# A fused two-block transformer on one core: activations placed at the top of SBUF, weight slots picked by operand role, and six small tiles for the last stage's split gates

## The chip, the cores and the metric

The kernel runs on one core of a Trainium2 chip. The metric is the device time of one execution in microseconds, taken as the median of three runs. One further execution was recorded by the hardware profiler, and the rows in this document come from that one.

## What is computed

The reference is two model blocks in a row on 256 tokens of width 1024, all in float32. The first block is a SwiGLU layer, a mixer (stick-breaking attention and a state-space scan side by side), a cross attention on 256 memory rows, and a second SwiGLU layer. The second block is a convolution and a gated recurrence, and then a layer of 16,384 small experts, which takes nearly half of the time. Cut to that layer:

```python
q = (xt @ wq).reshape(t, PEER_HEADS, 2, HALF_Q)
scores = jnp.einsum('thpd,hpnd->thpn', q, keys)
...                                   # top 16 of 16 x 16 sums per head: expert ids and gates
def block(args):
    u = jnp.take(u_tab, eb, axis=0)
    a = gelu(jnp.einsum('td,thkd->thk', xb, u))
    w = gb * a
    vv = jnp.take(v_tab, eb, axis=0)
    return jnp.einsum('thk,thkd->td', w, vv)
```

The kernel doesn't gather. It multiplies all tokens with the whole table u, scales the result by a matrix of gates that is zero for experts not chosen, and multiplies that with the whole table v.

## The kernel before

All weights arrive as 533 *units* of 128 x 1024 floats, in the order in which they are needed. SyncE loads a unit into a raw buffer. `prefetch` then takes a free *slot*: ScalarE writes the rounded value into its `hi` tile (L142), VectorE the rest into its `lo` tile (L143). So each product of two floats becomes three matmuls (high x high, high x low, low x high) on operands that TensorE takes in one pass. Activations are split in the same way, into `uT0` (high) and `uT1` (low), or into blocks of the arena `ra`.

A matmul has two operands in SBUF: the one that is loaded into the array first (here called the *held* operand) and the one that is streamed through it. There are two ways to use a weight unit:

- `f_tile` (L305 to L307) holds the weights and streams the activations, 256 columns: 24 matmuls a unit. The projections that come out by feature use it, most of the SwiGLU units, 12 units of the experts' query (`pq`), and all 128 units of the u table (`pu`).
- `half_chunk` (L272 to L276) and `acc_step` (L322 to L326) hold the activations and stream the weights, 512 columns. The last 128 units (`pv`, the v table) are of this kind: 12 matmuls a unit into four accumulators.

There are eight slots in SBUF (`hi0`/`lo0` to `hi7`/`lo7`), two more in `ra` for a while, and only slots 0 to 3 from `pq` on. A slot becomes free when its unit has been used up (`release`); `prefetch` takes `max(slots)`.

Where a tile lies follows from the order in which the pools allocate. In KB from the start of a partition, by the program's own memory table:

| tile | before | after |
|---|---|---|
| `raw0`; `raw1`, `raw2` | 18; 22 to 30 | 18; 216 to 224 |
| slots 0 to 3 | 30 to 62 | 22 to 54 |
| `uT0`, `uT1` (activations) | 62 to 78 | 200 to 216 |
| slots 4 to 7 | 88 to 120 | 129 to 161 |
| `fa` (float32 arena) | 120 to 185 | 64 to 129 |
| `ra` (split arena, two extra slots) | 185 to 217 | 161 to 193 |
| `X` (experts' matrix, last stages) | 80 to 208 | 68 to 196 |
| `w0`, `w1` (first split gates) | 212 to 216 | 56 to 60 |
| `r00` to `r31` (split gates) | none | 60 to 68 |

Below, *low* means slots 0 to 3 and all else under 78 KB, and *high* means 86 KB and above; before, TensorE reads no matmul operand in between.

In the `pu` stage VectorE and GpSimd work beside TensorE: first they pick experts (`routing`), then `gates` builds 64 groups of gates and scales `X` with them. In the `pv` stage `wsplit(i + 4)` (L1473, L1474) splits the gated matrix `X` four units ahead, into the eight places of `uT`, which is free by then; units 0 and 1 use `w0`/`w1`.

The order of all instructions is the order in which this Python code issues them: each helper calls `tick`, which may call `prefetch` or a step of a side task.

Of the kernel before, what the change touches and what calls it, by code (L numbers as in the profile page):

```python
# [5 lines left out]
F32 = mybir.dt.float32  # L6
F32R = mybir.dt.float32r
# [8 lines left out]
D = 1024  # L16
# [3 lines left out]
UNITS = [("ff1", 66), ("v", 8), ("qk", 16), ("dt", 1), ("xs", 8), ("bc", 4), ("z", 8),  # L20
         ("mk", 8), ("wo1", 16), ("mv", 8), ("xq", 8), ("xo", 8), ("ff2", 66),
         ("v2", 4), ("g2", 4), ("f2", 4), ("q2", 4), ("chb", 12), ("wo2", 8),
         ("pq", 16), ("pu", 128), ("pv", 128)]
FIRST = {}
# [10 lines left out]
FFN_AT = {}  # L35
_n = 0
for _s in FFN_ORDER:
    FFN_AT[_s] = _n
    _n += 4 if _s[0] == "gu" else 2

COLS = [("ffn1_pre_g", 8), ("mix_pre_g", 8), ("xa_pre_g", 8), ("mem_g", 8), ("ffn2_pre_g", 8),
        ("norm_mix_2", 8), ("norm_ffn_2", 8), ("attn_norm_g", 8), ("ssd_norm_g", 8), ("conv_gain_2", 4),
# [9 lines left out]
ROWS = ["ffn1_post_g", "mix_post_g", "xa_post_g", "ffn2_post_g", "norm_f_2", "d_skip"]  # L52
# [48 lines left out]
class Builder:  # L101
    RAW = 3
    RING = (4, 4)

    def __init__(self, tc, io, dbg=None, stop=None):
        self.tc, self.nc, self.io = tc, tc.nc, io
# [6 lines left out]
        self.retired = False  # L113
        self.live = sum(self.RING)
        self.sides = []
# [11 lines left out]
    def prefetch(self, n=1):  # L127

        nc = self.nc
        self.load()  # L130
        while n > 0 and self.split_i < self.dma_i:
            i = self.split_i
            slots = [x for x in self.free if x < self.RING[0] or i < FIRST["pq"]]
            if not slots:
                return
            slot = max(slots)
            self.free.remove(slot)
            self.slot_of[i] = slot
            hi, lo = self.slots[slot]
            x = self.raw_of.pop(i)  # L140
            raw = self.raw[x]
            nc.scalar.activation(hi, raw, AF.Copy)  # L142
            nc.vector.tensor_sub(lo, raw, hi.bitcast(F32))  # L143
            self.split_i += 1
            if x < self.RAW or not self.retired:
                self.raw_free.append(x)
            else:
                self.raw_extra.pop(x).free()
            n -= 1
            self.load()  # L150
# [31 lines left out]
    def retire(self, slots=True):  # L182

        self.retired = True
        if slots:
            self.live = sum(self.RING)
        for slot in [x for x in self.free if x >= self.live]:
# [1150 lines left out]

    def gates(self, kT, X):

# [33 lines left out]

    def peer(self):
        nc, hT = self.nc, self.uT
        small_scope = self.tc.tile_pool(name="px", bufs=1)
        px = small_scope.__enter__()
        X = px.tile([128, 128, 256], F32, name="X")
        XA = Arena(X.rearrange("p i t -> p (i t)")[:, 40 * 256:], 88 * 256)  # L1380
        kT = px.tile([128, 4, 256], F32, name="kT")
# [83 lines left out]
                self.u_done = i + 1  # L1465
            return f
        self.routed = False
        w01 = tuple(px.tile([128, 2, 256], F32R, name=f"w{i}") for i in range(2))

        def wsplit(i):  # L1470
            if i < 128:
                wh, wl = (p[:, i % 8] for p in (hT if i > 1 else w01))
                nc.scalar.activation(wh, X[:, i], AF.Copy)  # L1473
                nc.vector.tensor_sub(wl, X[:, i], wh.bitcast(F32))  # L1474
        for i in range(128):
# [8 lines left out]
        if not early:  # L1484
# [2 lines left out]
        h_scope.__exit__(None, None, None)  # L1487
        v_scope = self.tc.tile_pool(name="pv", bufs=1)
        pv = v_scope.__enter__()
        row = pv.tile([128, D], F32, name="nf")  # L1490
        src = self.io["rows"]
        nc.scalar.dma_start(row, bass.AP(tensor=src.tensor, offset=src.offset + ROWS.index("norm_f_2") * D,
                                         ap=[[0, 128], [1, D]]))
        hs = [slice(i * 512, i * 512 + 512) for i in range(2)]

        def done(t):
# [19 lines left out]
        tail = 2  # L1516
        for i in range(128 - tail):
            wsplit(i + 4)
            w = self.get(FIRST["pv"] + i)
            for t in range(2):  # L1520
                self.acc_step(i % 8 if i > 1 else i, t, w, hT if i > 1 else w01, False, False)
            self.release(FIRST["pv"] + i)
            self.tick(2.6)
        ends = [done(t) for t in range(2)]
        for t, halves in ((0, (0, 1)), (1, (0,)), (1, (1,))):
            for i in range(128 - tail, 128):
                self.acc_step(i % 8, t, self.get(FIRST["pv"] + i), hT, False, i == 127, halves)
            for j in ((0, 0), (1, 0), (1, 1))[t + halves[0]]:
                next(ends[j])
        v_scope.__exit__(None, None, None)  # L1530
        small_scope.__exit__(None, None, None)


    def build(self):
        tc, nc, io = self.tc, self.nc, self.io
        from contextlib import ExitStack
        with ExitStack() as top:
            top.enter_context(tc.manual_schedule())
            pool = lambda name, **kw: top.enter_context(tc.tile_pool(name=name, bufs=1, **kw))
            self.const = pool("const")  # L1540
            st = pool("stream")
            self.small = top.enter_context(tc.tile_pool(name="small", bufs=3))
            ps = pool("psum", space=bass.MemoryType.PSUM)
            self.acc = [ps.tile([128, 512], F32, name=f"acc{i}") for i in range(4)]
            self.mmb = [ps.tile([128, 512], F32, name=f"mm{i}") for i in range(2)]
            self.sdb = [ps.tile([128, 512], F32, name=f"sd{i}") for i in range(2)]
            self.cols = self.const.tile([128, N_COLS], F32, name="cols")
            mk = lambda p, i: (p.tile([128, 1024], F32R, name=f"hi{i}"), p.tile([128, 1024], F32R, name=f"lo{i}"))
            self.raw = [st.tile([128, 1024], F32, name=f"raw{i}") for i in range(self.RAW)]
            self.slots = [mk(st, i) for i in range(self.RING[0])]  # L1550
            self.uT = tuple(st.tile([128, 8, 256], F32R, name=f"uT{i}") for i in range(2))
            with ExitStack() as early:
                ep = early.enter_context(tc.tile_pool(name="early", bufs=1))
                self.h = ep.tile([128, 2, 1024], F32, name="h")
                for i in range(2):
                    nc.sync.dma_start(self.h[:, 0, i * 512:i * 512 + 512], io["x"][0:128, i * 512:i * 512 + 512])
                nc.sync.dma_start(self.cols, io["cols"])
                self.slots += [mk(ep, self.RING[0] + i) for i in range(self.RING[1])]
                self.free = list(range(len(self.slots)))
                fa = ep.tile([128, self.FN], F32, name="fa")  # L1560
                ra = ep.tile([128, self.RN], F32R, name="ra")
                self.FA, self.RA = Arena(fa, self.FN), Arena(ra, self.RN)
                self.junk = early.enter_context(tc.tile_pool(name="junk", bufs=1))
                self.load()
                nc.sync.dma_start(self.h[:, 1, :], io["x"][128:256])
                self.hold = None
                self.load()
                self.early = ep
                self.constants()
                self.seg = ep.tile([128, 256], F32, name="seg")  # L1570
                nc.gpsimd.memset(self.seg, 1.0)
                nc.gpsimd.memset(self.seg.rearrange("p (n c) -> p n c", c=32)[:, :, 0:1], 0.0)
                hb = self.FA.alloc(128)
                hm = hb.ap
                nc.gpsimd.memset(hm, 1.0)
                nc.gpsimd.affine_select(hm, hm, pattern=[[1, 128]], base=0, channel_multiplier=-1,
                                        compare_op=OP.is_ge, fill=0.0)
                nc.gpsimd.affine_select(hm.rearrange("p (n c) -> p n c", c=32), hm.rearrange("p (n c) -> p n c", c=32),
                                        pattern=[[-32, 4], [0, 32]], base=0, channel_multiplier=1,
                                        compare_op=OP.is_ge, fill=0.0)  # L1580
                self.hmask = ep.tile([128, 128], U32, name="hmask")
                nc.vector.tensor_copy(self.hmask, hm)
                hb.free()

                if self.first_half():
                    return
                self.live = self.RING[0]
                self.free = [x for x in self.free if x < self.RING[0]]
            self.iota = self.const.tile([128, 128], F16, name="iota")
            nc.gpsimd.iota(self.iota, pattern=[[1, 128]], base=0, channel_multiplier=0,  # L1590
                           allow_small_or_imprecise_dtypes=True)
            self.peer()
# [171 lines left out]
```

## Time and profile before

| | us |
|---|---|
| median of three runs | 1668.2 (1668.09 to 1668.7) |
| the profiled execution | 1668.19 |
| its span, first to last instruction | 1666.5 |
| TensorE busy | 1646.7 |
| VectorE busy | 1152.9 |
| ScalarE busy | 980.3 |
| GpSimd busy | 270.4 |

The span is what the rows of the trace cover; 1.7 us of the profiled execution lie around it. Matmuls overlap, so the distance from one matmul's start to the next is a better measure of their pace than the duration that a row gives.

### The profile page before, as it was taken

What the parts mean: (1) busy time and instruction counts of PE and PEld (TensorE: products, weight loads), DVE (VectorE), ACT (ScalarE), POOL (GpSimd) and SP (SyncE); (2) the same over time, 40 slices, a digit from 0 to 9 for tenths busy, and PEclk for the clock granted to TensorE, in tenths of its full rate; (3) what the DMA queues carried; (4) which work ended last, traced back from release to release, by engine and by line L of the source; (5) the groups of instructions that cost most, each with busy time, mean ns of one, the idle gap of its engine ahead of it and who ended that gap; (6) DMA issues with size and microseconds to landing.
All of it is one profiled execution on the core that took longest, in us unless ns stands there. A gap on an engine that the chain in (4) does not pass through costs nothing.

```text
span 1666.5 us, 29156 instructions
## 1 busy us (share of the span) xinstructions
PE 1646.7 (99%) x11102; PEld 1498.7 (90%) x11102; DVE 1152.9 (69%) x2366; ACT 980.3 (59%) x1826; POOL 270.4 (16%) x311
## 2 busy tenths in 40 slices
PE   7999999999999999999999999999999999999998
PEld 6999899988898899989889999999999888888886
DVE  7555565777756755567657998899999855555554
ACT  7444476786555644456355554888877645545544
POOL 0000000000000000000100002988888100000000
PEclk9999999999999999999999999999999999999999
DMA  9555443254535755526244555444444555555553
GB/s 329 195 200 188 150 141 127 104 201 152 175 104 166 274 182 200 190 100 202 79 138 153 178 179 188 154 164 165 165 153 160 193 193 191 197 192 192 196 194 127
DMA packets 79325, 288.77 MB, mean 173 GB/s; under 512 B 8784, under 2 KB 8912, under 8 KB 79056
## 3 DMA queue, kind: packets, MB, share of 16 engines
q1 hardware_dynamic: 77904, 281.66, 49.1%
q10 hardware_dynamic: 1280, 5.24, 0.8%
q8 instruction: 87, 1.43, 0.3%
q14 instruction: 54, 0.44, 0.1%
HBM read 285.82 MB, written 1.05 MB: 172 GB/s over the span
## 4 chain that ended last, share of the span: by engine, by line
PE 93%; DVE 3%; ACT 1%; issue 1%; DMA 1%; POOL 0%; SPq 0%; POOLq 0%; DVEq 0%; ACTq 0%
PE mm L305 15%; PE mm L306 15%; PE mm L307 15%; PE acc L322 11%; PE acc L324 11%; PE acc L326 11%; PE mm L276 2%; PE mm L273 2%; PE mm L272 2%; PE sd L1361 2%; DVE lo L143 1%; PE sd L383 1%; DMA raw<-ws 1%; PE acc L585 1%; PE sd L1416 0%
## 5 line engine op out<-in xcount | busy, mean ns | idle before, releaser
L143 DVE TENSOR_TENSOR lo<-raw,hi 128x1024 fp32r<-128x1024 f32 x419 | 513.2, 1228 | 265.7 <-ACT hi L142 263.2
L305 PE MATMUL mm<-uT,hi 128*128 128x256 f32 x2024 | 580.8, 287 | 2.1 <-DVE X L1464 1.0
L306 PE MATMUL mm<-uT,hi 128*128 128x256 f32 x2024 | 571.2, 282 | 0.0
L307 PE MATMUL mm<-uT,lo 128*128 128x256 f32 x2024 | 571.1, 282 | 0.0
L142 ACT ACTIVATE hi<-raw 128x1024 fp32r<-128x1024 f32 x419 | 442.1, 1058 | 218.3 <-PE acc L326 185.6
L305 PEld LDWEIGHTS mm<-uT,hi 128*128 128x128 f32 x2024 | 385.9, 191 | 4.3 <-DVE X L1464 1.6
L306 PEld LDWEIGHTS mm<-uT,hi 128*128 128x128 f32 x2024 | 386.1, 191 | 0.8
L307 PEld LDWEIGHTS mm<-uT,lo 128*128 128x128 f32 x2024 | 385.9, 191 | 0.0
L1348 POOL TENSOR_SCALAR m<-iota,kT 128x128 f16<-128x128 f16 x256 | 232.3, 924 | 205.6 <-DVE kT L1331 154.2
L322 PE MATMUL acc<-hi,uT 128*128 128x512 f32 x536 | 166.3, 391 | 0.0
L324 PE MATMUL acc<-lo,uT 128*128 128x512 f32 x536 | 165.5, 389 | 0.0
L326 PE MATMUL acc<-hi,uT 128*128 128x512 f32 x536 | 165.4, 389 | 0.0
L411 POOL TENSOR_TENSOR hr<-hv,mhalf 128x1 f32<-128x1 f32 x26 | 15.2, 585 | 817.9 <-DVE hv L410 817.9
L143 DVE TENSOR_TENSOR lo<-fa,hi 128x1024 fp32r<-128x1024 f32 x74 | 90.1, 1224 | 65.6 <-ACT hi L142 65.0
L324 PEld LDWEIGHTS acc<-lo,uT 128*128 128x128 f32 x536 | 100.6, 188 | 21.1
L322 PEld LDWEIGHTS acc<-hi,uT 128*128 128x128 f32 x536 | 100.4, 188 | 21.2 <-issue 0.5
L326 PEld LDWEIGHTS acc<-hi,uT 128*128 128x128 f32 x536 | 100.6, 188 | 21.0
L142 ACT ACTIVATE hi<-fa 128x1024 fp32r<-128x1024 f32 x74 | 77.4, 1055 | 43.3 <-PE mm L306 24.4
L1461 ACT ACTIVATE X<-mm 128x256 f32<-128x256 f32 (+40 forms) x126 | 39.8, 316 | 106.4 <-PE mm L307 105.6
L1350 ACT ACTIVATE oh<-m,kT 128x128 f16<-128x128 f16 x256 | 81.1, 390 | 0.0
L322 PE MATMUL acc<-hi,ra 128*128 128x512 f32 x216 | 71.0, 410 | 0.6 <-ACT ra L1169 0.6
L324 PE MATMUL acc<-lo,ra 128*128 128x512 f32 x216 | 67.3, 393 | 0.0
(358 smaller groups left out, 2351.5 us busy)
## 6 DMA issues: line engine op xcount, KB each, us to landing
raw<-ws SPq DMA_DIRECT2D x443, 512.0 KB, 3.3
fa<-ws SPq DMA_DIRECT2D x90, 512.0 KB, 3.3
fa<-rows ACTq DMA_DIRECT2D x5, 512.0 KB, 4.1
fa<-mem ACTq DMA_DIRECT2D x1, 1024.0 KB, 7.6
X<-keysT ACTq DMA_DIRECT2D x1, 1024.0 KB, 4.8
out<-X SPq DMA_DIRECT2D x4, 256.0 KB, 2.1
h<-x SPq DMA_DIRECT2D x2, 256.0 KB, 2.9
h<-x SPq DMA_DIRECT2D x1, 512.0 KB, 7.7
```

What stands on the lines that cost most here:

```text
L142: nc.scalar.activation(hi, raw, AF.Copy)
L143: nc.vector.tensor_sub(lo, raw, hi.bitcast(F32))
L272: nc.tensor.matmul(ps, ah[:, k, ts], wh, start=(k == 0), stop=False)
L305: nc.tensor.matmul(ps, wh, ah[:, k, :], start=(k == 0), stop=False)
L306: nc.tensor.matmul(ps, wh, al[:, k, :], start=False, stop=False)
L307: nc.tensor.matmul(ps, wl, ah[:, k, :], start=False, stop=(k == 7))
L322: nc.tensor.matmul(o[h], ah[:, k, ts], hi[:, hs[h]], start=first, stop=False)
L324: nc.tensor.matmul(o[h], ah[:, k, ts], lo[:, hs[h]], start=False, stop=False)
L326: nc.tensor.matmul(o[h], al[:, k, ts], hi[:, hs[h]], start=False, stop=last)
L1348: nc.gpsimd.tensor_scalar(m1[:, i], self.iota, key(0, i), None, op0=OP.is_equal)
L1350: nc.scalar.activation(oh[:, i], m1[:, i], AF.Copy, scale=key(2, i))
L1461: nc.scalar.activation(X[:, i, g:256], ps[:, g:256], AF.Gelu)
```

## The change

The pools are opened in another order and from another end, so that the activations come to lie at the top of SBUF, and the table above changes. `prefetch` gets a set `HELD` of units whose weights are the held operand, and gives these the lowest free slot, the others the highest. In the last stage the split gates no longer use `uT`: `w0`/`w1` and four pairs of small tiles (`r00` to `r31`, of 1 KB each) make a ring of six places; they lie where the gates' own buffers were. The row of final gains (`nf`) loses its tile: it is loaded into a used-up piece of `X` after unit 16.

```diff
+HELD = set()
+for _name in ("qk", "dt", "xs", "bc", "mk", "xq", "f2", "q2", "chb", "pu"):
+    HELD |= set(range(FIRST[_name], FIRST[_name] + dict(UNITS)[_name]))
+HELD |= set(range(FIRST["pq"] + 4, FIRST["pq"] + 16))
+for _name in ("ff1", "ff2"):
+    for _s, _at in FFN_AT.items():
+        if _s[0] == "gu" and _s[1] > 1:
+            HELD |= set(range(FIRST[_name] + _at, FIRST[_name] + _at + 4))
...
-            slot = max(slots)
+            slot = min(slots) if i in HELD else max(slots)
...
-        small_scope = self.tc.tile_pool(name="px", bufs=1)
+        small_scope = self.tc.tile_pool(name="px", bufs=1, side="right")
         px = small_scope.__enter__()
+        left_scope = self.tc.tile_pool(name="pl", bufs=1)
+        pl = left_scope.__enter__()
...
-        w01 = tuple(px.tile([128, 2, 256], F32R, name=f"w{i}") for i in range(2))
+        w01 = tuple(pl.tile([128, 2, 256], F32R, name=f"w{i}") for i in range(2))
+        ring = []
+
+        def wpart(i):
+
+            j = i % (2 + len(ring))
+            return (w01, j) if j < 2 else (ring[j - 2], 0)
...
-                wh, wl = (p[:, i % 8] for p in (hT if i > 1 else w01))
+                parts, j = wpart(i)
+                wh, wl = (p[:, j] for p in parts)
...
-        row = pv.tile([128, D], F32, name="nf")
+        ring.extend(tuple(pv.tile([128, 1, 256], F32R, name=f"r{j}{i}") for i in range(2)) for j in range(self.VRING))
+        row = X[:, 12:16].rearrange("p a b -> p (a b)")
         src = self.io["rows"]
-        nc.scalar.dma_start(row, ...)
...
         for i in range(128 - tail):
             wsplit(i + 4)
+            if i == 16:
+                nc.scalar.dma_start(row, ...)
...
-            self.raw = [st.tile([128, 1024], F32, name=f"raw{i}") for i in range(self.RAW)]
+            right = top.enter_context(tc.tile_pool(name="right", bufs=1, side="right"))
+            self.uT = tuple(right.tile([128, 8, 256], F32R, name=f"uT{i}") for i in range(2))
+            self.raw = [(right if i else st).tile([128, 1024], F32, name=f"raw{i}") for i in range(self.RAW)]
             self.slots = [mk(st, i) for i in range(self.RING[0])]
-            self.uT = tuple(st.tile([128, 8, 256], F32R, name=f"uT{i}") for i in range(2))
...
+                fa = ep.tile([128, self.FN], F32, name="fa")
                 self.slots += [mk(ep, self.RING[0] + i) for i in range(self.RING[1])]
                 self.free = list(range(len(self.slots)))
-                fa = ep.tile([128, self.FN], F32, name="fa")
```

No engine has a step more or less than before, and the matmuls follow each other in the same order. Two places show what does move. In these rows a matmul is written as output, then the streamed and the held operand; lines of the changed kernel lie 11 to 20 further down, and the number behind the underscore only tells tiles apart.

TensorE in the first SwiGLU layer, where unit 55 (slot 4) ends and unit 56 (slot 3) begins, before:

```order
1042 L306 MATMUL mm0_73<-uT1_90,hi4_98 128x256
1043 L307 MATMUL mm0_73<-uT0_89,lo4_99 128x256
1044 L305 MATMUL mm0_73<-uT0_89,hi4_98 128x256
1045 L306 MATMUL mm0_73<-uT1_90,hi4_98 128x256
1046 L307 MATMUL mm0_73<-uT0_89,lo4_99 128x256
1047 L305 MATMUL mm1_74<-uT0_89,hi3_87 128x256
1048 L306 MATMUL mm1_74<-uT1_90,hi3_87 128x256
1049 L307 MATMUL mm1_74<-uT0_89,lo3_88 128x256
```

The same place with the change:

```order
1042 L317 MATMUL mm0_73<-uT1_82,hi4_102 128x256
1043 L318 MATMUL mm0_73<-uT0_81,lo4_103 128x256
1044 L316 MATMUL mm0_73<-uT0_81,hi4_102 128x256
1045 L317 MATMUL mm0_73<-uT1_82,hi4_102 128x256
1046 L318 MATMUL mm0_73<-uT0_81,lo4_103 128x256
1047 L316 MATMUL mm1_74<-uT0_81,hi3_92 128x256
1048 L317 MATMUL mm1_74<-uT1_82,hi3_92 128x256
1049 L318 MATMUL mm1_74<-uT0_81,lo3_93 128x256
```

Both units stand in `HELD`, and both keep their slots: as a rule only one slot is free when `prefetch` asks, so lowest and highest are the same one. Through the whole program the same slots or their neighbours are taken, and no unit goes from slots 0 to 3 to a higher one or back. What has moved is `uT`, from the low side to the high one.

ScalarE where the last stage begins, with the split gates (L1473, then L1493) between the weight units (L142, then L153), before:

```order
1149 L1473 ACTIVATE w0_8108<-X_7590 128x256 x2
1150 L1463 ACTIVATE mm1_74<-mm1_74 128x256
1151 L142 ACTIVATE hi0_81<-raw0_78 128x1024
1152 L1492 DMA nf_14059<-rows 128x1024
1153 L1473 ACTIVATE uT0_89<-X_7590 128x256 x3
1154 L142 ACTIVATE hi2_85<-raw1_79 128x1024
1155 L1473 ACTIVATE uT0_89<-X_7590 128x256
1156 L142 ACTIVATE hi1_83<-raw2_80 128x1024
1157 L1473 ACTIVATE uT0_89<-X_7590 128x256
```

The same place with the change:

```order
1149 L1493 ACTIVATE w0_8114<-X_7596 128x256 x2
1150 L1476 ACTIVATE mm1_74<-mm1_74 128x256
1151 L153 ACTIVATE hi0_86<-raw0_83 128x1024
1152 L1493 ACTIVATE r00_14065<-X_7596 128x256
1153 L1493 ACTIVATE r10_14067<-X_7596 128x256
1154 L1493 ACTIVATE r20_14069<-X_7596 128x256
1155 L153 ACTIVATE hi1_88<-raw1_84 128x1024
1156 L1493 ACTIVATE r30_14071<-X_7596 128x256
1157 L153 ACTIVATE hi2_90<-raw2_85 128x1024
1158 L1493 ACTIVATE w0_8114<-X_7596 128x256
```

The steps are the same ones in the same order; the split gates go to other tiles, the place of unit 0 is written again for unit 6, and the load of the gains' row is gone from here (it comes 16 units later).

## Rows read from the trace of the kernel before

**Rows 1.** The page: span, busy time, granted clock (tenths), chain by engine.

```profile
span 1666.5 us, 29156 instructions
...
PE 1646.7 (99%) x11102; PEld 1498.7 (90%) x11102; DVE 1152.9 (69%) x2366; ACT 980.3 (59%) x1826; POOL 270.4 (16%) x311
...
PEclk9999999999999999999999999999999999999999
...
PE 93%; DVE 3%; ACT 1%; issue 1%; DMA 1%; POOL 0%; SPq 0%; POOLq 0%; DVEq 0%; ACTq 0%
```

**Rows 2.** Timeline of TensorE, first SwiGLU layer: first matmul of units 52, 56, 59.

```profile
160.63 0.28 PE L305 MATMUL mm<-uT,hi 128*128 128x256 f32 x1
...
171.99 0.28 PE L305 MATMUL mm<-uT,hi 128*128 128x256 f32 x1
...
180.63 0.28 PE L305 MATMUL mm<-uT,hi 128*128 128x256 f32 x1
```

**Rows 3.** Timeline of TensorE, memory keys: matmuls 2 and 24 of two units.

```profile
368.24 0.28 PE L306 MATMUL mm<-ra,hi 128*128 128x256 f32 x1
...
370.87 0.28 PE L307 MATMUL mm<-ra,lo 128*128 128x256 f32 x1
...
382.50 0.28 PE L306 MATMUL mm<-ra,hi 128*128 128x256 f32 x1
...
385.07 0.27 PE L307 MATMUL mm<-ra,lo 128*128 128x256 f32 x1
```

**Rows 4.** Timeline of TensorE where the last stage begins.

```profile
1311.86 0.63 PE L322 MATMUL acc<-hi,w 128*128 128x512 f32 x2
...
1314.65 0.63 PE L322 MATMUL acc<-hi,w 128*128 128x512 f32 x2
...
1317.45 0.62 PE L322 MATMUL acc<-hi,uT 128*128 128x512 f32 x2
...
1321.54 0.62 PE L322 MATMUL acc<-hi,uT 128*128 128x512 f32 x2
```

**Rows 5.** Stretches, matmuls of L305 alone: busy time and count on TensorE.

```profile
868.00:1165.00 297.00, 218.07 (x761) 145.57 (x761) 1.00 0.50 171
1165.00:1312.00 147.00, 102.64 (x354) 67.42 (x353) 1.00 0.47 158
```

**Rows 6.** Stretches of the u table: us, then PE, PEld, DVE, ACT, POOL busy.

```profile
925.60:940.00 14.40, 14.40 (x122) 14.40 (x122) 14.02 (x73) 7.69 (x13) 0.00 (x0) 1.00 0.56 199
...
968.80:983.20 14.40, 14.40 (x122) 14.40 (x122) 14.32 (x68) 7.68 (x13) 0.00 (x0) 1.00 0.60 203
...
1164.80:1181.20 16.40, 16.40 (x154) 16.23 (x154) 16.14 (x47) 13.46 (x35) 14.45 (x17) 1.00 0.46 162
1181.20:1197.60 16.40, 16.40 (x154) 16.23 (x154) 15.89 (x47) 12.81 (x35) 13.65 (x16) 1.00 0.47 161
1197.60:1214.00 16.40, 16.40 (x154) 16.23 (x154) 16.40 (x47) 13.17 (x36) 14.78 (x17) 1.00 0.47 152
...
1279.60:1296.00 16.40, 15.98 (x146) 15.35 (x146) 16.40 (x46) 11.56 (x33) 13.39 (x16) 1.00 0.48 157
1296.00:1312.40 16.40, 16.14 (x141) 15.79 (x140) 15.99 (x33) 10.55 (x28) 2.67 (x4) 1.00 0.48 166
```

**Rows 7.** TensorE's waits from 870 to 1320 us: total, times, longest.

```profile
PE mm L305 <- DVE X L1464: 1.0, 3, 0.4
```

**Rows 8.** Timeline, last stage: unit 6's gates are split (ScalarE, VectorE) and used.

```profile
1317.65 1.06 ACT L142 ACTIVATE hi<-raw 128x1024 fp32r<-128x1024 f32 x1 [1.44 <-PE acc L326]
1318.62 0.40 ACT L1473 ACTIVATE uT<-X 128x256 fp32r<-128x256 f32 x1
...
1319.89 0.42 DVE L1474 TENSOR_TENSOR uT<-X,uT 128x256 fp32r<-128x256 f32 x1
...
1328.34 0.62 PE L322 MATMUL acc<-hi,uT 128*128 128x512 f32 x2
```

**Rows 9.** DMA issues: the row of final gains (us to landing last).

```profile
nf<-rows ACTq DMA_DIRECT2D x1, 512.0 KB, 5.1
```

More of the change, by code (lines that the diff above doesn't have):

```diff
@@ L103 @@
     RING = (4, 4)
+    VRING = 4
     def __init__(self, tc, io, dbg=None, stop=None):
@@ L1489, in peer @@
         pv = v_scope.__enter__()
-        row = pv.tile([128, D], F32, name="nf")
+        ring.extend(tuple(pv.tile([128, 1, 256], F32R, name=f"r{j}{i}") for i in range(2)) for j in range(self.VRING))
+        row = X[:, 12:16].rearrange("p a b -> p (a b)")
         src = self.io["rows"]
-        nc.scalar.dma_start(row, bass.AP(tensor=src.tensor, offset=src.offset + ROWS.index("norm_f_2") * D,
-                                         ap=[[0, 128], [1, D]]))
         hs = [slice(i * 512, i * 512 + 512) for i in range(2)]
@@ L1518, in peer @@
             wsplit(i + 4)
+            if i == 16:
+                nc.scalar.dma_start(row, bass.AP(tensor=src.tensor, offset=src.offset + ROWS.index("norm_f_2") * D,
+                                                 ap=[[0, 128], [1, D]]))
             w = self.get(FIRST["pv"] + i)
+            parts, j = wpart(i)
             for t in range(2):
-                self.acc_step(i % 8 if i > 1 else i, t, w, hT if i > 1 else w01, False, False)
+                self.acc_step(j, t, w, parts, False, False)
             self.release(FIRST["pv"] + i)
@@ L1526, in peer @@
             for i in range(128 - tail, 128):
-                self.acc_step(i % 8, t, self.get(FIRST["pv"] + i), hT, False, i == 127, halves)
+                parts, j = wpart(i)
+                self.acc_step(j, t, self.get(FIRST["pv"] + i), parts, False, i == 127, halves)
             for j in ((0, 0), (1, 0), (1, 1))[t + halves[0]]:
@@ L1530, in peer @@
         v_scope.__exit__(None, None, None)
+        left_scope.__exit__(None, None, None)
         small_scope.__exit__(None, None, None)
```

## The prediction

> [...]
>
> [...] In the first SwiGLU layer units 52 to 55 lie in slots 7 to 4 and units 56 to 59 in slots 3 to 0; nothing else differs. The first four take 171.99 - 160.63 = 11.36 us for 96 matmuls, 118.3 ns each; the next three, 180.63 - 171.99 = 8.64 us for 72, 120.0 ns each [rows 2]. The streamed activations lay low (62 to 78 KB), so weights from the other side go faster. The mirror image stands in the memory keys, whose activations lie in `ra`, on the high side: the unit in slot 7 takes 370.87 - 368.24 = 2.63 us for 22 steps, 119.5 ns each, the unit in slot 3 385.07 - 382.50 = 2.57 us, 116.8 ns [rows 3]. So I read four prices for 256 columns: both operands on one side 120.0 (low) or about 119.5 to 120 (high), streamed low and held high 118.3, streamed high and held low 116.8.
>
> With 512 columns it is the other way round. The last stage begins with two units whose gates (`w`, high) are held against low weights: 24 matmuls in 1317.45 - 1311.86 = 5.59 us, 232.9 ns each; then the gates lie in `uT`, low, and 18 take 1321.54 - 1317.45 = 4.09 us, 227.2 ns [rows 4]. Here one side is 5.7 ns cheaper.
>
> [...] The rows say that a matmul's pace depends on where its two operands lie. [...]
>
> **The change, part by part.**
>
> *The table `HELD`: nothing.* By the order of the program only neighbouring slots change hands, and no unit changes sides, because mostly one slot is free at a time. All gain or loss comes from `uT`, which goes from low to high, and from the gates of the last stage.
>
> *Units used by `f_tile` before the experts' layer: -1.9 us.* I counted 129 such units that stream `uT`: 61 in slots 0 to 3, 68 in slots 4 to 7 or in `ra`. The 61 go from 120.0 to 116.8: 61 x 24 x 3.2 ns = 4.7 us gained. The 68 go from 118.3 to 120.0: 68 x 24 x 1.7 = 2.8 us lost. Low bound: if the new pairs get only the weaker of the two mixed prices (118.3), the gain is 2.5 us and the net a loss of 0.3.
>
> *512 columns: -0.7 us.* Of the matmuls that hold `uT`, 360 come from a mixed pair onto one side and 264 go the other way: 96 x 5.7 ns = 0.5 us. Those that hold `ra` keep their sides. The 24 of the last stage's first two units come onto one side: 0.1 us. The other matmuls of that stage held low tiles and still do, so its long part keeps 227.2 ns.
>
> *`pq` and `pu`, 140 units, all in slots 0 to 3: -8.1 us.* All go from 120.0 to 116.8, 77 ns a unit, as far as TensorE sets the pace. L305 runs eight times a unit, so 761 of them up to 1165 us are 95 units, worth 7.3 us; the 354 after that are 44 units, worth 3.4 us [rows 5]. But from 1165 us VectorE, which builds gates and splits weights there, is nearly full: 16.14 and 15.89 of 16.40, then six stretches at 16.40, and 15.99 in the last [rows 6]. All its idle time from 1164.8 to 1312.4 us is 0.26 + 0.51 + 0.41 = 1.2 us, and a faster TensorE can use no more than that; I take 0.8. Bounds: 10.8 us if VectorE gave way entirely, 3.9 + 0.8 = 4.7 us at the weaker price.
>
> *The ring of six places: nothing.* ScalarE splits unit 6 at 1318.62 us, VectorE at 1319.89, and it is used at 1328.34; its new place is that of unit 0, after which unit 1 begins at 1314.65 [rows 4, 8]. So the place is free 4 us before the split, and the split is ready 8 us before its use. Besides, ScalarE's step just ahead of it already waits for a later unit (1.44 us on L326) [rows 8], so no new wait can end last.
>
> *The row of gains: nothing.* The load goes from the stage's start to unit 16, still ahead of its use by 109 units; uncovered, it would cost its landing time, 5.1 us [rows 9]. `raw1` and `raw2` are no operands of TensorE.
>
> **Sum.** 1.9 + 0.7 + 8.1 = 10.7 us. The profiled execution took 1668.19 us, 1.7 more than its span; the median is 1668.2, so both give **1657.5 us**, 0.6% less.
>
> **Rivals.**
>
> 1. *VectorE takes more of the gain, or the new pair gets the weaker price: 1663 us.* VectorE is also full while experts are picked: 14.02 and 14.32 of 14.40 us [rows 6]. If it became the bound from 925 us on, only 18 units (12 of `pq`, 6 of `pu`) would gain their 77 ns, 1.4 us, plus some 1.6 us of its idle time: 1.9 + 0.7 + 3.0 = 5.6, so 1662.6. The weaker price gives -0.3 + 0.7 + 4.7 = 5.1, so 1663.1. Against the first: in the whole stretch TensorE waited three times for VectorE, 1.0 us in all [rows 7], and splits run up to three units ahead. Against the second: the mirror rows [rows 3] have just this pair of sides, if only with few matmuls.
> 2. *The new places don't count as two sides: 1670.3 us.* No row has weights at 22 KB or activations streamed from 200 to 216 KB. If 120.0 holds for every pair, the 68 units lose their 2.8 us, nothing else of 256 columns moves, and 512 columns give 0.7: 2.1 us slower, which counts as no change. [Rows 2] speak against it: one line, one stage, and only the slot differs. [...]
> 3. *Slower: the ring of six stalls the last stage.* If the split of unit i + 4 had to wait until its place is read, each of 126 units would wait on ScalarE and VectorE. From 85 ns a unit on this eats up the 10.7 us; at 0.2 us a unit it is 25 us and the time 1683. It decides only if the split came some 8 us later than now, which nothing in [rows 8] suggests.
>
> **How the numbers follow.** Forecast, from full VectorE freedom (1.9 + 0.7 + 10.8 = 13.4, so 1654.8) to 1661.5: 0.66. Rival 1: 0.18. Rival 2: 0.11. Rival 3: 0.05. The range 1654.5 to 1664.0 holds the first two. A run of this kernel can tell about 0.2%, 3.3 us, from no change; so faster 0.84, same 0.11, slower 0.05.
>
> **What would show it.** Right: in `pu`, starts of 24 matmuls 2.80 us apart instead of 2.88; in the first SwiGLU layer units 52 to 55 at 2.88 and 56 to 59 at 2.80, the reverse of now; the first 12 matmuls of the last stage at 227 ns; VectorE at 16.40 of 16.40 earlier than 1198 us, and more waits of L305's matmul for it; the last stage as long as now. Wrong: 2.88 us in `pu`, waits of L322's matmuls for the gates' split, or TensorE idle while experts are picked.

## The result: slower by 0.6%, and what the profile after shows

The changed kernel takes **1679.05 us** (median of four runs, 1678.47 to 1679.72) against 1668.45 for the kernel before beside it: a ratio of 1.0064, 95% interval 1.0046 to 1.0081. The forecast was 1657.5, so even the sign was wrong. The profiled execution took 1679.72 us.

The page after, same four lines as [rows 1]: span, busy time, granted clock, chain.

```profile
span 1678.0 us, 29155 instructions
...
PE 1658.4 (99%) x11102; PEld 1499.5 (89%) x11102; DVE 1154.0 (69%) x2366; ACT 980.6 (58%) x1826; POOL 268.0 (16%) x311
...
PEclk9999999999999999999999999999999999999999
...
PE 94%; DVE 3%; ACT 1%; DMA 1%; issue 1%; POOL 0%; SPq 0%; POOLq 0%; ACTq 0%; DVEq 0%
```

TensorE bounds both: 94% of the chain that ended last, after 93% [rows 1]. The granted clock is the same (9 in every slice of both pages), and VectorE and ScalarE did the same work (1154.0 and 980.6 us busy, after 1152.9 and 980.3). TensorE's busy time grew by 11.7 us and the span by 11.5. So matmuls follow each other more slowly somewhere. Where, the start of the last stage shows; this is TensorE's timeline, to be laid beside [rows 4].

```profile
1313.31 0.62 PE L333 MATMUL acc<-hi,w 128*128 128x512 f32 x2
...
1318.90 0.63 PE L333 MATMUL acc<-hi,r 128*128 128x512 f32 x2
...
1330.10 0.63 PE L333 MATMUL acc<-hi,w 128*128 128x512 f32 x2
```

Units 0 and 1, with the gates in `w`, take 5.59 us for 24 matmuls, 232.9 ns each, exactly as before. But units 2 to 5, with the gates in the new small tiles `r`, take 11.20 us for 48, 233.3 ns each, where `uT` gave 227.2. It stays so. Two windows of the stage (us; busy time and count on TensorE, PEld, VectorE, ScalarE, GpSimd; granted clock; DMA share; GB/s), first before, then after:

```profile
1340.00:1640.00 300.00, 300.00 (x1325) 248.40 (x1324) 171.96 (x221) 151.14 (x222) 0.00 (x0) 1.00 0.57 194
```

```profile
1340.00:1640.00 300.00, 300.00 (x1288) 241.54 (x1287) 167.53 (x215) 146.17 (x215) 0.00 (x0) 1.00 0.56 190
```

In the same 300 us TensorE begins 1288 matmuls instead of 1325: 232.9 against 226.4 ns. Over 1,512 matmuls (126 units of 12) 6.5 ns are 9.8 us, nearly the whole loss.

And the gain that was forecast for `pu` is not there. L316 alone (L305 before), to be laid beside [rows 5]:

```profile
868.00:1165.00 297.00, 217.09 (x759) 143.00 (x760) 1.00 0.50 171
1165.00:1312.00 147.00, 102.56 (x354) 66.45 (x354) 1.00 0.46 158
```

759 and 354 against 761 and 354: the u table goes at its old pace. Nor did the first SwiGLU layer turn round. Units 52, 56 and 59 start here, to be laid beside [rows 2]:

```profile
160.48 0.28 PE L316 MATMUL mm<-uT,hi 128*128 128x256 f32 x1
...
171.79 0.28 PE L316 MATMUL mm<-uT,hi 128*128 128x256 f32 x1
...
180.43 0.28 PE L316 MATMUL mm<-uT,hi 128*128 128x256 f32 x1
```

11.31 us for 96 matmuls (117.8 ns), then 8.64 for 72 (120.0 ns): `uT` went from one end of SBUF to the other, and each unit keeps its price within half a nanosecond.

No new wait has come in. From 1300 us on, TensorE's waits are one row, at the end of `pu`, and unit 6's gates (ScalarE, then VectorE) are ready at 1321.75, 8.3 us before their use at 1330.10, as in [rows 8]:

```profile
PE mm L316 <- DVE X L1477: 0.2, 1, 0.2
```

```profile
1320.06 0.40 ACT L1493 ACTIVATE w<-X 128x256 fp32r<-128x256 f32 x1
...
1321.33 0.42 DVE L1494 TENSOR_TENSOR w<-X,w 128x256 fp32r<-128x256 f32 x1
```

**A second look at the addresses.** The built programs give every tile's first byte in its partition. Rounded to KB, as in the table of the section on the kernel, they hide what follows from the small tiles ahead of each one: how many bytes it lies past a multiple of 256.

| kernel | slots 0-3 | slots 4-7, `ra`, `w`, `r` | `uT` | f_tile in `pu` | last stage |
|---|---|---|---|---|---|
| before | 128 | 160 | 128 | 0 | 0 |
| after | 128 | 160 | 224 | 160 | 32 |
| slots_up32 | 160 | 160 | 224 | 192 | 0 |
| uT_up32 | 128 | 160 | 160 | 224 | 32 |
| gates_in_uT | 128 | 160 | 224 | 160 | 96 |
| gates_down32 | 128 | 128 | 224 | 160 | 0 |
| offset64 | 32 | 32 | 224 | 64 | 0 |

The last two columns are the held operand's offset less the streamed one's, modulo 256; from here on that is *the difference*. Before the change, the tiles that I called low lay at 128 and those that I called high at 160. Side and offset said the same thing in every row that I had, and I had looked at one of them.

### The profile page after: what moved, and what is told of

Its sections match the earlier page's. It is cut to its first block, busy times and chain, and to the rows that moved or that the text cites. A ratio compares the mean times of both kernels' runs of the same rounds, so it can differ in the third digit from the quotient of the medians.

```text
span 1678.0 us, 29155 instructions
## 1 busy us (share of the span) xinstructions
PE 1658.4 (99%) x11102; PEld 1499.5 (89%) x11102; DVE 1154.0 (69%) x2366; ACT 980.6 (58%) x1826; POOL 268.0 (16%) x311
## 4 chain that ended last, share of the span: by engine, by line
PE 94%; DVE 3%; ACT 1%; DMA 1%; issue 1%; POOL 0%; SPq 0%; POOLq 0%; ACTq 0%; DVEq 0%
PE mm L316 15%; PE mm L318 15%; PE mm L317 15%; PE acc L333 11%; PE acc L335 11%; PE acc L337 11%; PE mm L287 3%; PE mm L283 3%; PE mm L284 3%; PE sd L1372 2%; DMA raw<-ws 1%; PE sd L394 1%; DVE lo L154 1%; PE acc L596 1%; ACT hi L153 0%
## 5 line engine op out<-in xcount | busy, mean ns | idle before, releaser
L316 PE MATMUL mm<-uT,hi 128*128 128x256 f32 x2024 | 578.7, 286 | 2.1 <-DVE X L1477 1.1
L153 ACT ACTIVATE hi<-raw 128x1024 fp32r<-128x1024 f32 x419 | 441.9, 1058 | 230.4 <-PE acc L337 193.8
L316 PEld LDWEIGHTS mm<-uT,hi 128*128 128x128 f32 x2024 | 381.2, 188 | 4.3 <-DVE X L1477 1.8
L317 PEld LDWEIGHTS mm<-uT,hi 128*128 128x128 f32 x2024 | 382.2, 189 | 0.8
L318 PEld LDWEIGHTS mm<-uT,lo 128*128 128x128 f32 x2024 | 379.4, 187 | 0.0
L333 PE MATMUL acc<-hi,r 128*128 128x512 f32 x336 | 105.5, 396 | 0.0
L335 PE MATMUL acc<-lo,r 128*128 128x512 f32 x336 | 105.5, 396 | 0.0
L337 PE MATMUL acc<-hi,r 128*128 128x512 f32 x336 | 105.4, 396 | 0.0
L153 ACT ACTIVATE hi<-fa 128x1024 fp32r<-128x1024 f32 x74 | 77.4, 1055 | 43.2 <-PE mm L317 24.3
L333 PEld LDWEIGHTS acc<-hi,r 128*128 128x128 f32 x336 | 63.1, 188 | 15.3
L337 PEld LDWEIGHTS acc<-hi,r 128*128 128x128 f32 x336 | 63.1, 188 | 15.2
L335 PEld LDWEIGHTS acc<-lo,r 128*128 128x128 f32 x336 | 63.1, 188 | 15.2
```

What stands on the lines that cost most here:

```text
L316: nc.tensor.matmul(ps, wh, ah[:, k, :], start=(k == 0), stop=False)
L317: nc.tensor.matmul(ps, wh, al[:, k, :], start=False, stop=False)
L318: nc.tensor.matmul(ps, wl, ah[:, k, :], start=False, stop=(k == 7))
L333: nc.tensor.matmul(o[h], ah[:, k, ts], hi[:, hs[h]], start=first, stop=False)
L335: nc.tensor.matmul(o[h], ah[:, k, ts], lo[:, hs[h]], start=False, stop=False)
L337: nc.tensor.matmul(o[h], al[:, k, ts], hi[:, hs[h]], start=False, stop=last)
```

## Experiments

**Theory A**: the pace depends on the difference and on nothing else of the place. **Theory B**: it depends on where in SBUF the tiles lie. **Theory C**: the small tiles of the last stage cost something as such. Theories D and E stand in the texts below.

### slots_up32: the changed kernel, eight floats of padding

```diff
-            sm = self.small.tile([128, 8], F32, name="gsm", bufs=2)
+            sm = self.small.tile([128, 8], F32, name="gsm", bufs=1)
...
+            st.tile([128, 8], F32, name="pad")
             self.slots = [mk(st, i) for i in range(self.RING[0])]
```

The pad (`pad`) moves slots 0 to 3 by 32 bytes. The edit of `gsm` takes 32 bytes away behind them, so that every tile after it keeps its place.

> The changed kernel with slots 0 to 3 moved up by 32 bytes, so that they and the small tiles of the split gates start at the same offset within 256 bytes (a scratch tile of 32 bytes is dropped behind them, so that everything else stays). Theory A (what counts is the difference of the two operands' byte offsets within some small block: 512-column matmuls take 227 ns at equal offsets and 233 otherwise): the last stage falls from 358 to 348 us, the layers before lose some 2 us, the u table some 5, and the time is about 1661 us (1657 to 1669). Theory B (what counts is which part of SBUF the operands lie in): 32 bytes change no side, 1679 us. Theory C (six small tiles cost more than one large): the last stage stays at 358 us, 1679 us.

Measured: **1659.77 us** (1659.28 to 1661.39) beside 1668.88; ratio 0.9946 (0.993 to 0.9963). 32 bytes turn the loss of 10.6 us into a gain of 9.1. The windows show both halves, the old pace in the last stage and more matmuls in the u table; the third row is the u table of the changed kernel:

```profile
1340.00:1640.00 300.00, 300.00 (x1325) 248.41 (x1324) 172.47 (x222) 150.47 (x221) 0.00 (x0) 1.00 0.57 195
925.00:1045.00 120.00, 120.00 (x1033) 119.87 (x1032) 110.14 (x362) 69.59 (x115) 18.86 (x19) 1.00 0.55 185
...
925.00:1045.00 120.00, 120.00 (x1007) 119.95 (x1006) 108.80 (x361) 65.38 (x104) 13.58 (x13) 1.00 0.53 185
```

B and C fall.

### uT_up32: the kernel before, the same pad ahead of `uT`

> The kernel before with uT alone moved up by 32 bytes. Theory A: the last stage, where the gates lie in uT, rises from 348 to 357 us (233 ns instead of 227), while the 256-column matmuls on slots 0 to 3 fall from 120 to 117 ns, so that the query and the u table up to the gates lose some 4 us; about 1670 us in all (1667 to 1673). Theory B: 1668 us, each stage as before. Theory C says nothing of it: 1668 us.

Measured: **1669.56 us** (1668.55 to 1670.71), ratio 1.0004 (0.9995 to 1.0014). Two large effects cancel, as A said: the last stage, whose steps, tiles and KB are those of before, takes 10.1 us more, and the stages from `pq` to the end of `pu` 7.1 less.

```profile
1340.00:1640.00 300.00, 300.00 (x1288) 241.70 (x1286) 167.58 (x215) 146.13 (x215) 0.00 (x0) 1.00 0.55 188
925.00:1045.00 120.00, 120.00 (x1042) 119.88 (x1041) 111.15 (x366) 71.15 (x120) 21.25 (x20) 1.00 0.56 187
```

1288 is the changed kernel's count, in a kernel that has none of the change.

### gates_in_uT: the changed kernel, gates of the last stage back in `uT`

```diff
-            j = i % (2 + len(ring))
-            return (w01, j) if j < 2 else (ring[j - 2], 0)
+            return (hT, i % 8) if i > 1 else (w01, i)
...
-        ring.extend(tuple(pv.tile([128, 1, 256], F32R, name=f"r{j}{i}") for i in range(2)) for j in range(self.VRING))
```

> The changed kernel with the split gates of units 2 to 127 back in uT, which lies at the top of SBUF. Theory A: uT has another offset than slots 0 to 3, so the last stage stays at 358 us and the time at 1679. Theory B with two sides: gates high, weights low, 233 ns as well, 1679 us. Theory C: the small tiles are gone and the last stage returns to 348 us, 1669 us.

Measured: **1681.38 us** (1680.48 to 1682.45), ratio 1.0079 (1.0062 to 1.0095). The small tiles are not to blame. The last stage is 1.4 us longer still than in the changed kernel (1282 matmuls in the 300 us, 234.0 ns); its difference is 96 now, and the next run has a price for that.

```profile
1340.00:1640.00 300.00, 300.00 (x1282) 241.20 (x1281) 166.41 (x214) 145.80 (x213) 0.00 (x0) 1.00 0.56 188
```

### sweep: matmuls alone

A program of matmuls back to back, which doesn't compute the model. Each of its lines is one block of 96 matmuls of 256 columns, or 48 of 512, in the order high x high, high x low, low x high; the numbers are the columns and the bytes added to the held and to the streamed operand's start.

```diff
+        for a, b, first, last in plan(lowh, lows, 512, 32, 0):
+            nc.tensor.matmul(acc[0][:, 0:512], a, b, start=first, stop=last)
```

> Matmuls alone, not the model: 96 with 256 columns or 48 with 512 at each of 30 placements of the held against the streamed operand. Theory A: at equal offsets 120 and 227 ns whether the two lie 10 KB or 120 KB apart; at a difference of 32 bytes 118 and 233 ns, at 224 bytes 117 and 233; 256 bytes as equal or not tells the block's size. Theory B: the offset in bytes does nothing, and the pairs far apart differ from the near ones by 6 ns at 512 columns. Theory C says nothing of it.

The timeline has a row for a block, so the next row's start less its own, over the count, is the pace. 256 columns with differences of 0, 16, 32, 48, 64 and 96 (95 matmuls each; the first one of each block stands alone at the start of the timeline), then 512 columns with 0, 16, 32 and 48, then 512 columns with 0, 32 and 224 and the held tiles some 120 KB further up:

```profile
48.46 11.55 PE L50 MATMUL acc<-streamedlow,heldlow 128*128 128x256 f32 x95
59.85 11.40 PE L52 MATMUL acc<-streamedlow,heldlow 128*128 128x256 f32 x95
71.09 11.39 PE L54 MATMUL acc<-streamedlow,heldlow 128*128 128x256 f32 x95
82.32 11.87 PE L56 MATMUL acc<-streamedlow,heldlow 128*128 128x256 f32 x95
94.03 10.94 PE L58 MATMUL acc<-streamedlow,heldlow 128*128 128x256 f32 x95
104.80 11.56 PE L60 MATMUL acc<-streamedlow,heldlow 128*128 128x256 f32 x95
...
184.47 11.05 PE L74 MATMUL acc<-streamedlow,heldlow 128*128 128x512 f32 x48
195.36 11.05 PE L76 MATMUL acc<-streamedlow,heldlow 128*128 128x512 f32 x48
206.25 11.35 PE L78 MATMUL acc<-streamedlow,heldlow 128*128 128x512 f32 x48
217.44 11.36 PE L80 MATMUL acc<-streamedlow,heldlow 128*128 128x512 f32 x48
...
351.76 11.06 PE L104 MATMUL acc<-streamedlow,heldhigh 128*128 128x512 f32 x48
362.66 11.35 PE L106 MATMUL acc<-streamedlow,heldhigh 128*128 128x512 f32 x48
373.85 11.36 PE L108 MATMUL acc<-streamedlow,heldhigh 128*128 128x512 f32 x48
```

So 512 columns: 195.36 - 184.47 = 10.89 us, 226.9 ns, with a difference of 0; 217.44 - 206.25 = 11.19, 233.1 ns, with 32; the same with the held tiles far away (10.90 and 11.19). All points, in ns:

| difference | 0 | 16 | 32 | 48 | 64 | 96 | 128 | 160 | 192 | 224 | 256 | 288 |
|---|---|---|---|---|---|---|---|---|---|---|---|---|
| 256 columns | 120 | 118 | 118.3 | 123 | 113.4 | 120 | 119 | 120.0 | 117.8 | 117.8 | 119.9 | 118.3 |
| 512 columns | 226.9 | 226.7 | 233.2 | 233.3 | 233.2 | 234.2 | 232.4 | 233.4 | 229.1 | 233.4 | 226.7 | 233.2 |

Where it was measured past 256 bytes it repeats: 256 and 288 gave 119.9 and 118.3 ns, and 226.7 and 233.2, as 0 and 32 did (120 and 118.3, 226.9 and 233.2). Both operands moved by 32 bytes: 119.8 and 226.9. The streamed operand alone moved by 32 bytes, a difference of 224: 116.7, so at 224 there are two values. Distance in SBUF changed nothing in this sweep (119.8, 118.3 and 116.7 for 0, 32 and 224 with the held tiles far away, all of them values that near tiles gave too). That settles A against B without the kernel around it.

### gates_down32, no_held and offset64

Three more versions of the changed kernel. In `gates_down32` the first edit of `slots_up32` stands alone: all that lies behind that scratch tile comes down by 32 bytes, the gates among it.

> The changed kernel with one buffer less for a scratch tile of 32 bytes (gsm), nothing else: all tiles behind it move down by 32 bytes, among them the last stage's small gate tiles, slots 4 to 7 and ra; slots 0 to 3 and uT stay. Theory A (byte offset modulo 256): the last stage's gates now have the offset of the weights, so its 512-column matmuls go from 233 to 227 ns and the stage from 358 to 348 us, while slots 4 to 7 lose (117.7 to 120 ns, 68 units, 3.8 us) and 512 columns in the early stages gain some 2 us: prices times counts give 8 us less than the changed kernel, so 1671 (1668 to 1674). Theory B (places low or high) and theory C (the small tiles as such cost): as the changed kernel, 1679.

Measured: **1673.19 us** (1671.62 to 1673.57), ratio 1.0024 (1.0015 to 1.0033). One buffer less for a scratch tile of 32 bytes gives back 5.9 us; the last stage is back at its old pace, with the ring of six in place.

```profile
1340.00:1640.00 300.00, 300.00 (x1325) 248.47 (x1325) 172.04 (x221) 151.04 (x222) 0.00 (x0) 1.00 0.62 195
```

`no_held` drops the new choice of slots:

```diff
-            slot = min(slots) if i in HELD else max(slots)
+            slot = max(slots)
```

> The changed kernel without the table HELD's effect: prefetch takes the highest free slot for every unit, as before the change. All slots 0 to 3 have one byte offset and slots 4 to 7 another, and no unit goes from one group to the other, so theory A expects the changed kernel's time, 1679 (1677 to 1681). Theory E (the choice of slots changes when slots come free, and so the weights' arrival): some other time, by 3 us or more either way, with TensorE waiting on the slots' splits.

Measured: **1679.15 us** (1678.31 to 1679.94), ratio 1.0063 (1.0048 to 1.0079): nothing, as A and the prediction had it, and E falls.

`offset64` puts the sweep's best pair to use, a difference of 64 in all f_tile units that stream `uT` and 0 in the last stage:

```diff
-        v = self.small.tile([128, 32], F32, name="rv")[:, :w]
-        r = self.small.tile([128, 32], F32, name="rr", bufs=6)[:, :w]
+        v = self.small.tile([128, 32], F32, name="rv", bufs=2)[:, :w]
+        r = self.small.tile([128, 32], F32, name="rr", bufs=5)[:, :w]
...
-            sm = self.small.tile([128, 8], F32, name="gsm", bufs=2)
+            sm = self.small.tile([128, 8], F32, name="gsm", bufs=1)
...
+            st.tile([128, 40], F32, name="pad")
             self.slots = [mk(st, i) for i in range(self.RING[0])]
```

> The changed kernel with a pad of 160 bytes ahead of the weight slots, and 288 bytes less of small scratch tiles behind them (one gsm instead of two, five rr instead of six, two rv instead of three). By that the slots, ra and the last stage's gates all start 32 bytes past a multiple of 256, and uT 224 past one: for f_tile the held weights lie 64 bytes past the streamed activations modulo 256, for the last stage the difference is 0. Theory A (only that difference counts, at the prices of the run of matmuls alone: 113.5 ns for 256 columns at 64, 226.9 for 512 columns at 0, 229.1 at 192): the matmuls' prices times their counts fall from 1503.2 us (before) to 1461.7, 41 us; of that the stretch of 147 us in which VectorE has no room (7 us) can't be had, and a part of 3 to 8 us where experts are picked, so 1634 us, between 1628 and 1645. Units of the first SwiGLU layer should take 24 x 113.5 = 2.72 us, and the last stage as long as before (348 us). Theory B (low or high places count, not bytes): as the changed kernel, 1679. Theory D (offsets count, but VectorE sets the pace of the whole u table already): 1648 to 1652.

Measured: **1645.47 us** (1643.91 to 1648.59), ratio 0.986 (0.9845 to 0.9875): the best version here, 23.1 us under the kernel before, though just outside what A expected (1628 to 1645). D falls too, though the profiled execution (1648.59 us) lies in its range: from `pq` to the end of `pu` that execution is 10.7 us shorter, so VectorE does not set the pace of the whole table. Where the missing part went is in the timeline. Here are two stretches of `pu`'s first units, 54 matmuls and 33, both on the same `uT` and slots 0 to 3:

```profile
875.38 0.28 PE L316 MATMUL mm<-uT,hi 128*128 128x256 f32 x1
...
881.50 0.28 PE L316 MATMUL mm<-uT,hi 128*128 128x256 f32 x1
...
899.87 0.28 PE L316 MATMUL mm<-uT,hi 128*128 128x256 f32 x1
...
903.75 0.28 PE L316 MATMUL mm<-uT,hi 128*128 128x256 f32 x1
```

6.12 us over 54 are 113.3 ns, 3.88 over 33 are 117.6. Each stretch goes over more than one unit, and units write into `mm0` and `mm1` in turn, so the output tile does not choose the pace here. In this trace about half of the f_tile matmuls that stream `uT` (3,300 of 6,456 by their units' median) run at the second pace, all of both SwiGLU layers among them; at 4.4 ns that is 14.5 us. Another part is lost in `pu`'s last third: 44 units of 24 matmuls at 6.5 ns would be 6.9 us, and 1.3 came. There TensorE's waits from 1165 to 1320 us show VectorE late by 3.3 us in all, where it was 1.0 [rows 7].

```profile
PE mm L316 <- DVE X L1477: 2.1, 6, 0.5
PE sd L1372 <- DVE ol L1364: 1.2, 4, 0.4
```

The same third as windows (TensorE, PEld, VectorE, ScalarE, GpSimd), before and then in `offset64`, where the same matmuls run earlier:

```profile
1165.00:1312.00 147.00, 145.93 (x1335) 143.20 (x1334) 145.82 (x388) 111.38 (x299) 113.50 (x127) 1.00 0.47 158
...
1146.80:1292.40 145.60, 142.30 (x1335) 138.37 (x1333) 145.34 (x390) 111.67 (x299) 116.26 (x128) 1.00 0.49 159
```

VectorE was idle for 1.2 us there and is idle for 0.3 now; TensorE stands still for 3.3 us instead of 1.1.

### sweep_fine: what chooses between 113.3 and 117.8

Another program of matmuls alone, which doesn't compute the model either.

> Matmuls alone again, back to back (not the model), to see why units with a difference of 64 bytes run at 113.3 ns in some stages of the kernel offset64 and at 117.8 ns in others, with the same addresses. First 256 columns with the held operand 40 to 112 bytes past the streamed one, in steps of 4 to 24 bytes; then a difference of 64 after blocks with differences of 0, 160 and 32 and after blocks of 512 columns; then 64 with both operands 96 bytes further (the offsets that offset64 has); then 512 columns in small steps around 0 and 192. If the price depends on the difference alone, every block at 64 takes 113.5 ns. If absolute offsets count, the two blocks 96 bytes further take 117.8 and the others 113.5. If the pace is a state that lasts until something breaks the stream, blocks at 64 take 113.3 or 117.8 by what ran ahead of them. Around 0, 512 columns should take 226.9 ns up to a difference of 16 and 233 from some step between 16 and 32.

256 columns with a difference of 64 stand at L78 (behind a block with 0), L82 (behind 160) and L90 (behind 512 columns with 0); at L100 also behind 512 columns with 0, but both operands 96 bytes further:

```profile
205.49 11.47 PE L78 MATMUL acc<-streamedlow,heldlow 128*128 128x256 f32 x96
216.80 11.67 PE L80 MATMUL acc<-streamedlow,heldlow 128*128 128x256 f32 x96
228.31 11.05 PE L82 MATMUL acc<-streamedlow,heldlow 128*128 128x256 f32 x96
239.19 11.52 PE L84 MATMUL acc<-streamedlow,heldlow 128*128 128x256 f32 x96
...
272.34 11.47 PE L90 MATMUL acc<-streamedlow,heldlow 128*128 128x256 f32 x96
283.64 11.36 PE L92 MATMUL acc<-streamedlow,heldlow 128*128 128x512 f32 x48
...
327.57 11.04 PE L100 MATMUL acc<-streamedlow,heldlow 128*128 128x256 f32 x96
338.45 11.32 PE L102 MATMUL acc<-streamedlow,heldlow 128*128 128x512 f32 x48
```

117.8, 113.3, 117.7 and 113.3 ns. L78 and L82 read the same operands at the same addresses; what ran ahead of them differs, and so does the accumulator (`acc[0]` and `acc[2]`). This program can't part these two: its blocks at 64 into `acc[0]` and `acc[6]` were slow, and those into the others fast. In `offset64` both output tiles have both paces, as shown above, so there the tile is not what chooses. So in these runs a difference of 64 had two paces, 113.3 and 117.6 to 117.8 ns: they are the means of whole blocks of 96 here, and in `offset64` a stream kept one for 54 matmuls and the other for 33. What picks it isn't settled: L90 and L100 had the same kind of block ahead of them. So theory A holds for the loss (priced +11.1 us, measured +10.6, in the table below) and for the 512 columns of these runs, but for 256 columns at 64 (113.3 or 117.8) and, by 1.1 ns, at 224 (116.7 or 117.8) the difference alone doesn't give the price. Nor does every small step behave as a multiple of 32 does: 52 and 88 bytes also gave 113.4 and 113.6 ns, while 56 and 60 gave 117.8 and 119.6; 512 columns took 232.4 at a difference of 4 and 233.3 at 12, so the cheap value at 0 and 16 (226.9 and 226.7) is not a plateau, as I had expected.

## Why the prediction was wrong, point by point

The sweep's prices times each program's matmul counts by difference ("priced", with 116.7 ns for 224 and 113.4 for 64), and the measured changes, against the kernel before in us. The stages come from the profiled executions: the start of matmul n in the one less that in the other, at stage borders, over TensorE's 11,102 matmuls. The borders are the first `f_tile` matmul of `pq` and the first matmul of the last stage.

| kernel | priced | measured | layers before `pq` | `pq`, `pu` | last stage |
|---|---|---|---|---|---|
| after | +11.1 | +10.6 | +1.3 | +0.4 | +10.1 |
| no_held | +11.1 | +10.6 | +1.3 | +0.2 | +10.1 |
| gates_in_uT | +12.6 | +12.5 | +0.8 | +0.3 | +11.5 |
| gates_down32 | +3.5 | +4.7 | +4.8 | +0.8 | -0.1 |
| uT_up32 | -3.9 | +0.7 | -2.5 | -7.1 | +10.1 |
| slots_up32 | -11.3 | -9.1 | -1.9 | -4.8 | -0.1 |
| offset64 | -42.2 | -23.1 | -8.7 | -10.7 | -0.1 |

- **The step that failed** is reading [rows 2 to 4] as prices by side. "Only the slot differs" was not so, since slots 4 to 7 differ from slots 0 to 3 by 32 bytes of offset as well as by 58 KB. The prices themselves were read rightly, and all fit the difference: 32 is 118.3 and 0 is 120.0 [rows 2], 224 is 116.8 [rows 3], 32 is 232.9 and 0 is 227.2 [rows 4].
- ***`pq` and `pu`: -8.1 us.*** It was +0.4. The step took low weights under a high stream to be the fast pair (116.8); the new pair's difference is 160, which costs what 0 costs, 120.0. In `uT_up32`, with 224, the predicted price does appear, and the gain of 7.1 comes close to the 8.1; its part after the gates' start is small, as the term on VectorE said.
- ***512 columns: -0.7 us, and the last stage "keeps 227.2 ns".*** This is the costliest miss, +10.1 us: the stage was called unmoved because gates and weights both lay low. They went from a difference of 0 to 32. Its first 24 matmuls stayed at 32 and gained nothing. Nor did the earlier layers give their 0.5 us: the 360 matmuls went from 224 to 64, which cost the same (233.4 and 233.2 ns), and the 264 went from 0 to 96 and lost 1.3 us.
- ***Units before the experts' layer: -1.9 us.*** The layers took 1.3 us more, but the units account for little of that. The 68 in slots 4 to 7 or `ra` went from 32 to 192 (118.3 to 117.8 ns) and gained 1.0 us, where the prediction had a loss of 2.8. The 61 in slots 0 to 3 went from 0 to 160 (120.0 both); their starts came 0.6 us later in all, where it had a gain of 4.7. The rest is the 1.3 us of the 264 matmuls above. These sums are of distances from one start to the next, matmul by matmul, in the two profiled executions.
- ***`HELD`, the ring of six, the row of gains: nothing.*** Right: `no_held` measures the first, the waits show no sign of the second, and `gates_down32` has the old last stage with both in place.
- **Rival 2** was right that the new places don't count as two sides, but not in its sum, 1670.3: it took the last stage as given, and had the 68 units lose 2.8 us.
- **The bound of VectorE** was never reached in the changed kernel: from 870 to 1320 us TensorE waited 1.1 us for it, after 1.0 [rows 7]. In `uT_up32` and `offset64` it shows as the term had it: `pu`'s last third gave 0.6 and 1.3 us, where 3.4 and 6.9 were priced, and in `offset64` the waits grew to 3.3 us and VectorE was busy for all but 0.3 us of that third. The term's 1.2 us of idle time is about what `offset64` got. That it is VectorE alone is argued from its busy time and these waits; no run took its work away. The second pace (14.5 us) and this third (5.6), which overlap by some 0.7 us, make up most of the 22.7 us by which the profiled execution of `offset64` (1648.59 us) falls short of its price.

## What to carry to other kernels

When rows differ by a tile's place, write down its whole address before naming the cause: KB, and the rest modulo 256, the step after which the prices of the sweep repeated. Two groups of tiles behind the same small tiles share an offset, so "which pool" and "which offset" look alike until 32 bytes of padding part them (here 1679.05 us became 1659.77 in `slots_up32`); that experiment costs one line, and should come before a change of layout. In a kernel that TensorE bounds with float32r operands, measure the pace by the difference of held and streamed operand, and choose it by that: here that was 0 for 512 columns (226.9 ns, 233.2 at 32) and 64 for 256 (113.3 or 117.8, 120.0 at 0). Then hold it when scratch tiles are added, since a tile ahead can move those behind it: one buffer of 32 bytes less gave 5.9 us in `gates_down32`.

## What was not expected of the hardware

In these runs the pace of float32r matmuls with new weights each time changed with the operands' relative byte offset: 226.7 to 234.2 ns for 512 columns, 113.3 to 123 for 256, and 256 and 288 bytes gave what 0 and 32 gave, within 0.2 ns. (In the trace of the kernel before such a matmul is one row, 2,216 at L305 for 277 units of 8; one on plain float32 operands is two, 32 at L953 for 16.) What helped one shape didn't help the other (64: 113.4 for 256 columns and 233.2 for 512; 0: 120.0 and 226.9). At a difference of 64 two paces were measured, 113.3 and 117.8, as means of blocks of 96 matmuls and over stretches of 54 and 33. What brings this about no run here shows.
